# Normaliser states, conditioning vectors and a norm vector moved as rows with one transpose

## The chip, the cores and the metric

The kernel runs on one core of a Trainium2 chip. The core has five engines that work side by side: TensorE (PE) for matmuls and transposes, VectorE (DVE), ScalarE (ACT) and GpSimd (POOL) for elementwise work, and SyncE (SP), which here issues every transfer between device memory and the core's own memory (SBUF). PE writes into PSUM banks, which VectorE or ScalarE empty. The metric is the device time of one execution in microseconds, lower is better.

## The reference, cut to what matters

One layer of a diffusion backbone runs over 1024 sample tokens and 128 prompt tokens. A conditioning vector per group gives shifts and scales (`silu(c) @ w_mod + b_mod`). The mixer is a bidirectional mLSTM branch beside an attention branch; a feed-forward part follows. The mLSTM walks over the tokens in pieces and carries a matrix state C (256 x 256), a normaliser n (256) and a stabiliser m for each of 4 heads and 2 directions:

```python
num = w_inter[..., None] * jnp.einsum('bhid,bhde->bhie', qc, C) + jnp.einsum('bhij,bhje->bhie', s, vc)
den = w_inter * jnp.einsum('bhid,bhd->bhi', qc, n) + jnp.sum(s, -1)
h = num / jnp.maximum(jnp.abs(den), jnp.exp(-m_row))[..., None]
...
C_new = decay[..., None, None] * C + jnp.einsum('bhjd,bhje->bhde', wk, vc)
n_new = decay[..., None] * n + jnp.sum(wk, -2)
```

Sample tokens start from given states (`state_C`, `state_n`, `state_m`); prompt tokens start from zero, and their last states are outputs (`new_state_C`, `new_state_n` of shape 1 x 1 x 2 x 4 x 256, `new_state_m`). After the mLSTM each head's output is RMS-normalised and scaled by `mlstm_norm_g`, one number per channel.

## The kernel before, in words

**Layout.** The kernel keeps channels on the 128 partitions. A vector of 1024 numbers that is to lie with one number per partition and piece is read by the transfer in pieces of 4 bytes, since neighbours in memory go to different partitions. That holds for `mlstm_norm_g` into `mg` (line 393) and for each head's 256 numbers of `state_n` (line 514), and the other way for the final n into `o_n` (line 635). The conditioning vectors `c` and `c_ctx` lie with 8 neighbours on a partition, but go into `cT` with every second place (lines 298 and 299), again in pieces of 4 bytes. The modulation bias `b_mod` is read as 48 rows of 128 numbers into `bml` and transposed once on PE (line 330).

**A state tile.** C and n lie together in a tile `st` of 128 x 2 x 258: columns 0 to 255 are C, column 256 is n, column 257 is zero. The values `v` have a column of ones beside them, so one matmul group `kvp` updates C and n together. There are three `st` buffers in rotation.

**Stages.** Start (0 to about 60 us): modulation, transposes of x, gates. Then the mLSTM stage up to about 1000 us: `mlstm(h)` for the four heads in turn. Head h loads its backward state (`load_state(cur, h, 1)`), walks back over seven pieces and stores the state of each to device memory (`bs`), loads the forward state, and walks forward over eight sample pieces. The ninth piece is the prompt: for each direction its update is copied by ACT into an `st` buffer (`fin`, line 633) and stored, C in rows of 1 KB (`o_C`, line 634) and n from its column (`o_n`, line 635). `finish_h` transposes a piece's result on PE, scales it by `mg` on ACT (line 561) and stores it (`hmd`). Attention, the output projection and the feed-forward part follow.

**What sets the order.** `mlstm` is a generator. At each of its `yield`s the main loop takes a measured amount of other matmuls from `filler()` (projections `g`, copied out of PSUM by VectorE as `kvs` or `fm`, and late modulation pieces `mod_late`), so PE always has filler between the steps of the recurrence. The projections have two PSUM banks. A scheduler then fixes each engine's order once; an engine runs its list strictly in order. SP's list too: a transfer that has to wait holds all that come behind it. Transfers take their completion signals from a ring of eight, so each also waits until the eighth before it has landed.

**End of the mLSTM stage.** `prologue()` loads the keys `kTd` of the attention into `pe` tiles; ACT and VectorE split them into `kh` and `kl`. These loads stand on SP behind the last stores of the mLSTM stage.

**Statistics of the last norm.** `stats_act` uses four small tiles of 128 x 1, two buffers each.

Of the kernel before, what the change touches and what calls it, by code (L numbers as in the profile page):

```python
# [9 lines left out]
F32 = mybir.dt.float32  # L10
# [6 lines left out]
KT = 8  # L17
# [19 lines left out]
def hybrid_step_kernel(  # L37
# [27 lines left out]
    def load(out, in_):  # L65
        nc.sync.dma_start(out=out, in_=in_)

    def store(out, in_):
        nc.sync.dma_start(out=out, in_=in_)
# [63 lines left out]
    sc2p = cst.tile([128, 8, 2], F32, name="sc2p")  # L133
    bmT = cst.tile([128, 48], F32, name="bmT")
    silu = cst.tile([128, KT, 32], F32, name="silu")
    mg = cst.tile([128, 8], F32, name="mg")
    gq = cst.tile([128, 128], F32, name="gq")
    gk = cst.tile([128, 128], F32, name="gk")
    tmA = cst.tile([128, NT, 4, 4], F32, name="tmA")
# [46 lines left out]
    def ttile(shape):  # L186
        return ps1.tile(list(shape), F32, tag="t", bufs=1, name="pt")
# [106 lines left out]

    with ExitStack() as s0:
        p0 = pool(s0, "p0", 1)
        cT = p0.tile([128, KT, 2], F32, name="cT")
        load(cT[:, :, 0:1], c.rearrange("b (p k) -> p k b", k=KT))
        load(cT[:, :, 1:2], c_ctx.rearrange("(p k o) -> p k o", k=KT, o=1))
        sg = p0.tile([128, KT, 2], F32, name="sg")  # L300
        nc.scalar.activation(out=sg[:], in_=cT[:], func=AF.Sigmoid)
        nc.vector.tensor_tensor(out=silu[:, :, 0:2], in0=cT[:], in1=sg[:], op=ALU.mult)
        bml = p0.tile([48, 128], F32, name="bml")

        def mod_load(n, q):
            ch = p0.tile([128, 4, 512], F32, tag="ch", bufs=4, name="ch")
# [11 lines left out]

        c0 = [mod_load(0, q) for q in range(2)]
        load(sel[:], k_sel)  # L320
        load(bml[:], b_mod[0].rearrange("(j p) -> j p", p=128))
        load(ident[:], k_ident)
        c2 = [mod_load(2, q) for q in range(2)]
        load(wgr[:], kview(w_in)[:, :, GT:GT + 16])
# [1 line left out]
            load(bg[32 * j:32 * j + 4, :], b_gates[0, src:src + 4].rearrange("(p o) -> p o", o=1))  # L326
        for d in range(2):
            load(m0[32 * d:32 * d + 4, :], state_m[0, 0, d].rearrange("(p o) -> p o", o=1))
        pb = ttile([128, 48])
        nc.tensor.transpose(pb[:], bml[:], ident[0:48, 0:48])  # L330
        nc.vector.tensor_copy(out=bmT[:], in_=pb[:])
        mod_mm(0, c0)
        mod_mm(2, c2)
        nc.vector.tensor_scalar(sc1p[:, 0:4, :], modT[:, 8:12, :], 1.0, None, ALU.add)
# [55 lines left out]
            gate_mm(gg[b], b, range(4, KT), False, True)  # L390

    load(mask[:], k_mask)
    load(mg[:], mlstm_norm_g[0].rearrange("(k p) -> p k", p=128))
    load(gq[:], q_norm_g.partition_broadcast(128).rearrange("p o d -> p (o d)"))
    load(gk[:], k_norm_g.partition_broadcast(128).rearrange("p o d -> p (o d)"))
    nc.gpsimd.tensor_scalar(gq[:], gq[:], float(128.0 ** -0.5), None, ALU.mult)
# [92 lines left out]
    def mt(shape, tag, bufs=1, dt_=F32):  # L489
        return mp.tile(list(shape), dt_, tag=tag, bufs=bufs, name=tag)  # L490
# [20 lines left out]

    def load_state(dst, h, d):
        load(dst[:, :, 0:256], state_C[0, 0, d, h].rearrange("(k p) e -> p k e", p=128))
        load(dst[:, :, 256:257], state_n[0, 0, d, h].rearrange("(k p o) -> p k o", p=128, o=1))
        nc.gpsimd.memset(dst[:, :, 257:258], 0.0)

    def mlstm(h):
# [37 lines left out]
        def finish_h(s, hs):  # L555
            pt = ttile([128, 2, 128])
            for m in range(2):
                nc.tensor.transpose(pt[:, m, :], hs[:, 128 * m:128 * m + 128], ident[:])
            ho = mt([128, 2, 128], "ho", 2)
            for m in range(2):  # L560
                nc.scalar.activation(out=ho[:, m, :], in_=pt[:, m, :], func=AF.Copy, scale=mg[:, 2 * h + m:2 * h + m + 1])
            store(hmd[h][s][:], ho[:])
# [4 lines left out]
        for s in range(NT):  # L567
            sample = s < NS
            kv, v, uw, kT, pm = nxt_in
            qo = (s % 3) * 128  # L570
            q = qts[s // 3][:, :, qo:qo + 128]
            sp = ps1.tile([128, 512], F32, tag="s", bufs=1, name="sp")
            for m in range(2):
                nc.tensor.matmul(sp[:, 0:128], lhsT=kT[:, m, :], rhs=q[:, m, :], start=m == 0, stop=m == 1)
            sT = mt([128, 2, 128], "sT")
            nc.vector.tensor_tensor(out=sT[:], in0=sp[:, 0:128].unsqueeze(1).to_broadcast([128, 2, 128]), in1=pm[:], op=ALU.mult)
            sh, sl = mt([128, 2, 128], "sh", 1, F32R), mt([128, 2, 128], "sl", 1, F32R)
            split(sh[:], sl[:], sT[:])
            if sample:
                bw = mt([128, 2, 258], "bw", 2)  # L580
                load(bw[:], bsd[h][s][:])
                qw = mt([128, 2, 2, 128], "qw")
                nc.vector.tensor_tensor(out=qw[:], in0=q.unsqueeze(1).to_broadcast([128, 2, 2, 128]),
                                        in1=uw[:, 1, :, :].unsqueeze(2).to_broadcast([128, 2, 2, 128]), op=ALU.mult)
                qh, ql = mt([128, 2, 2, 128], "qh", 1, F32R), mt([128, 2, 2, 128], "ql", 1, F32R)
                split(qh[:], ql[:], qw[:])
                sts = []
                for nm, src in (("f", fw), ("b", bw)):
                    th, tl = mt([128, 2, 258], "sth" + nm, 1, F32R), mt([128, 2, 258], "stl" + nm, 1, F32R)
                    split(th[:], tl[:], src[:])  # L590
                    sts.append((th, tl))
            yield 1
            if pend is not None:
                finish_h(*pend)
            if s + 1 < NT:
                nxt_in = first(s + 1)
                yield 1
            op = ps1.tile([128, 2, 512], F32, tag="o", bufs=1, name="op")
            for d in range(2):
                terms = [((sh[:, d, :], sl[:, d, :]), (v[0][:], v[1][:]))]  # L600
                if sample:
                    terms += [((qh[:, d, m, :], ql[:, d, m, :]), (sts[d][0][:, m, :], sts[d][1][:, m, :])) for m in range(2)]
                mm3(op[:, d, 0:258], terms)
            r = mt([128, 2], "r", 2)
            nc.vector.tensor_tensor(out=r[:], in0=op[:, :, 256], in1=tmA[:, s, 2:4, h], op=ALU.max)
            nc.vector.scalar_tensor_tensor(out=r[:], in0=op[:, :, 256], scalar=-1.0, in1=r[:], op0=ALU.mult, op1=ALU.max)
            nc.vector.reciprocal(out=r[:], in_=r[:])
            ha = mt([128, 256], "ha")
            nc.scalar.activation(out=ha[:], in_=op[:, 0, 0:256], func=AF.Copy, scale=r[:, 0:1])
            hs = mt([128, 256], "hs", 2)  # L610
            nc.vector.scalar_tensor_tensor(out=hs[:], in0=op[:, 1, 0:256], scalar=r[:, 1:2], in1=ha[:], op0=ALU.mult, op1=ALU.add)
            ss = mt([128, 1], "ss", 2)
            jk = mt([128, 256], "jk")
            nc.scalar.activation(out=jk[:], in_=hs[:], func=AF.Square, scale=0.0625, accum_out=ss[:])
            nc.gpsimd.tensor_scalar(ss[:], ss[:], EPS, None, ALU.add)
            nc.gpsimd.tensor_tensor(out=ss[:], in0=ss[:], in1=mhalf[:, 0:1], op=ALU.pow)
            nc.vector.tensor_scalar(hs[:], hs[:], ss[:], None, ALU.mult)
            yield 1
            if sample:
                if s < NS - 1:  # L620
                    ps = kv_update(kv, v, h, s, 0)
                    nxt = mt([128, 2, 258], "st", 3)
                    for m in range(2):
                        nc.vector.scalar_tensor_tensor(out=nxt[:, m, :], in0=fw[:, m, :], scalar=dec[:, 0, h, s:s + 1],
                                                       in1=ps[m][:, 0:258], op0=ALU.mult, op1=ALU.add)
                    fw = nxt
                    yield 1
            else:
                for d in range(2):
                    ps = kv_update(kv, v, h, s, d)  # L630
                    fin = mt([128, 2, 258], "st", 3)
                    for m in range(2):
                        nc.scalar.activation(out=fin[:, m, :], in_=ps[m][:, 0:258], func=AF.Copy)
                    store(o_C[0, 0, d, h].rearrange("(k p) e -> p k e", p=128), fin[:, :, 0:256])
                    store(o_n[0, 0, d, h].rearrange("(k p o) -> p k o", p=128, o=1), fin[:, :, 256:257])
                    yield 1
            pend = (s, hs)
        finish_h(*pend)
        yield 1

# [515 lines left out]
        return nmu, rs, False  # L1156

    def stats_act(mk, y, jk):
        sm, nmu, ss, rs = (mk([128, 1], nm, 2) for nm in ("sm", "nmu", "sq", "brs"))
        nc.scalar.activation(out=jk, in_=y, func=AF.Copy, accum_out=sm[:])  # L1160
        nc.gpsimd.tensor_scalar(nmu[:], sm[:], -1.0 / D, None, ALU.mult)
        nc.scalar.activation(out=y, in_=y, func=AF.Identity, bias=nmu[:])
        nc.scalar.activation(out=jk, in_=y, func=AF.Square, accum_out=ss[:])
        nc.gpsimd.tensor_scalar(rs[:], ss[:], 1.0 / D, EPS, ALU.mult, ALU.add)
        nc.gpsimd.tensor_tensor(out=rs[:], in0=rs[:], in1=mhalf[:, 0:1], op=ALU.pow)
        return nmu, rs, True
# [334 lines left out]
```

## Time and profile before

| what | us |
|---|---|
| three runs | 2437.52, 2441.1, 2441.97 |
| median | 2441.1 |
| profiled execution, its own time | 2440.7 |
| its span, first to last instruction | 2438.9 |
| PE busy | 2360.1 (97%) |
| VectorE, ACT, POOL busy | 1495.6, 999.8, 366.6 |
| mean granted PE clock | 0.989 |
| PE busy in 0 to 60 us | 42.56 of 60 |
| PE busy in 300 to 400, 800 to 900, 1010 to 1100 us | 90.98 of 100, 91.38 of 100, 77.27 of 90 |

In the rows of the trace `out<-in` names what is written and read. L with a number is a line of the kernel before; lines 66 and 69 are the helpers `load` and `store`, 72 and 73 the helper `split`, 78 to 80 the three matmuls of `mm3`. `SPq` is SP's own queue. A wait row reads: who waited, for whom, us in total, times, longest. The windows give, for each stretch, length, busy time of PE, of PE's weight loads, VectorE, ACT and POOL with their instructions, then the granted PE clock (1 is full), the busy share of the 16 DMA engines and what they moved in GB/s.

### The profile page before, as it was taken

Reading aid. Unit: us, or ns where it says so; the run is one execution under the profiler, and the core shown is the slowest. Engines: PE = TensorE matmul, PEld = TensorE weight load, DVE = VectorE, ACT = ScalarE, POOL = GpSimd, SP = SyncE. Lnnn points to the kernel's source line nnn. Section 1 sums busy time; section 2 is a strip of 40 time slices with the busy share of each in tenths; the row PEclk is TensorE's granted clock in tenths of the full one; section 3 lists DMA queues with packets and bytes.
Section 4 is the critical chain, followed back from the end, with each engine's and each line's share of the span. In section 5 each row is a group of like instructions: output and inputs, shape, how many; then the busy total and the mean of one; then the engine's idle time right before and its main releaser. Section 6 shows DMA issues by size and latency. Waiting matters only on the chain.

```text
span 2438.9 us, 35985 instructions
## 1 busy us (share of the span) xinstructions
PE 2360.1 (97%) x13293; PEld 2135.6 (88%) x13293; DVE 1495.6 (61%) x2736; ACT 999.8 (41%) x2133; POOL 366.6 (15%) x566
## 2 busy tenths in 40 slices
PE   7999998999999899899999999999999999999997
PEld 4888887788899799898999999989999989999996
DVE  4745644745655455368788435679544587676777
ACT  3423432534433233246766423225433444444444
POOL 1000110201110011034444000010000121111111
PEclk9999999999999999999999999999999999999999
DMA  7265447445654653511000655434444452222222
GB/s 258 88 204 166 127 134 192 138 130 149 188 151 147 176 176 110 103 58 40 16 17 12 207 174 184 147 109 135 151 133 127 143 186 69 70 69 68 64 85 113
DMA packets 236849, 305.71 MB, mean 125 GB/s; under 512 B 25249, under 2 KB 175857, under 8 KB 236673
## 3 DMA queue, kind: packets, MB, share of 16 engines
q1 hardware_dynamic: 236672, 303.41, 41.2%
q8 instruction: 105, 1.72, 0.3%
q14 instruction: 72, 0.58, 0.1%
HBM read 236.55 MB, written 66.79 MB: 124 GB/s over the span
## 4 chain that ended last, share of the span: by engine, by line
PE 84%; DVE 6%; DMA 6%; ACT 2%; issue 1%; POOL 1%; SPq 0%; DVEq 0%; ACTq 0%; POOLq 0%
PE g L78 13%; PE g L80 13%; PE g L79 13%; PE u L1398 4%; PE d L78 3%; PE d L79 3%; PE d L80 3%; PE pz L1398 2%; PE pp L1398 2%; PE t L873 2%; PE u L80 2%; PE u L78 2%; PE u L79 2%; PE pa L79 2%; PE pa L80 2%; PE pa L78 2%
## 5 line engine op out<-in xcount | busy, mean ns | idle before, releaser
L78 PE MATMUL g<-th,wh 128*128 128x384 f32 x1088 | 373.6, 343 | 10.0 <-DVE fm L249 10.0
L80 PE MATMUL g<-th,wl 128*128 128x384 f32 x1088 | 368.2, 338 | 0.0
L79 PE MATMUL g<-tl,wh 128*128 128x384 f32 x1088 | 366.5, 337 | 0.0
L72 ACT ACTIVATE wh<-raw 128x1024 fp32r<-128x1024 f32 x180 | 188.7, 1057 | 316.2 <-PE d L80 142.3
L73 DVE TENSOR_TENSOR wl<-raw,wh 128x1024 fp32r<-128x1024 f32 x180 | 224.1, 1252 | 126.3 <-ACT wh L72 125.5
L78 PE MATMUL g<-wh,th 128*128 128x512 f32 x600 | 241.0, 402 | 0.3 <-DVE kvs L236 0.3
L79 PE MATMUL g<-wl,th 128*128 128x512 f32 x600 | 235.9, 393 | 0.2 <-DVE wl L73 0.2
L80 PE MATMUL g<-wh,tl 128*128 128x512 f32 x600 | 236.1, 394 | 0.0
L78 PEld LDWEIGHTS g<-th,wh 128*128 128x128 f32 x1088 | 206.4, 190 | 18.8 <-DVE fm L249 10.3
L79 PEld LDWEIGHTS g<-tl,wh 128*128 128x128 f32 x1088 | 206.5, 190 | 0.1
L80 PEld LDWEIGHTS g<-th,wl 128*128 128x128 f32 x1088 | 206.0, 189 | 0.4 <-issue 0.4
L1189 DVE TENSOR_TENSOR acc<-acc,d 128x512 f32<-128x512 f32 x160 | 109.5, 686 | 58.8 <-PE d L80 56.8
L78 PEld LDWEIGHTS g<-wh,th 128*128 128x128 f32 x600 | 113.1, 188 | 25.5 <-issue 3.8
L80 PEld LDWEIGHTS g<-wh,tl 128*128 128x128 f32 x600 | 113.0, 188 | 23.4
L79 PEld LDWEIGHTS g<-wl,th 128*128 128x128 f32 x600 | 113.2, 189 | 21.0 <-DVE wl L73 1.2
L72 ACT ACTIVATE ph<-t 128x384 fp32r<-128x384 f32 x192 | 91.0, 493 | 70.5 <-PE t L873 69.9
L249 DVE COPY fm<-g 128x384 f32<-128x384 f32 x96 | 53.2, 554 | 98.8 <-PE g L80 98.6
L73 DVE TENSOR_TENSOR pl<-t,ph 128x384 fp32r<-128x384 f32 x192 | 104.8, 549 | 9.0 <-ACT ph L72 7.2
L873 PE MATMUL t<-ident,pe 128*128 128x128 f32 x576 | 96.2, 276 | 6.3 <-DVE pl L73 5.4
L1302 POOL TENSOR_TENSOR wtl<-raw 128x512 f32<-128x512 f32 x16 | 21.2, 1324 | 487.4 <-PE pa L79 252.7
L862 POOL TENSOR_SCALAR pe<-pe,rs 128x1152 f32<-128x1152 f32 x64 | 79.0, 1234 | 54.8 <-DVE rs L861 26.9
L78 PE MATMUL pv<-ph,vh 128*128 128x256 f32 x288 | 85.6, 297 | 1.5 <-DVE tl L73 1.5
(392 smaller groups left out, 5905.5 us busy)
## 6 DMA issues: line engine op xcount, KB each, us to landing
raw<-in_w_up_dram SPq DMA_DIRECT2D x64, 512.0 KB
raw<-in_w_down_dram SPq DMA_DIRECT2D x64, 512.0 KB
raw<-in_w_in_dram SPq DMA_DIRECT2D x44, 512.0 KB
kvt<-kvd SPq DMA_DIRECT2D x64, 257.0 KB
raw<-in_w_mod_dram SPq DMA_DIRECT2D x32, 512.0 KB
kvd<-kvs SPq DMA_DIRECT2D x36, 257.0 KB
uw<-ud SPq DMA_DIRECT2D x72, 128.0 KB
bs<-st SPq DMA_DIRECT2D x32, 258.0 KB
```

Source lines behind the costliest of these rows:

```text
L72: nc.scalar.activation(out=hi, in_=src, func=AF.Copy)
L73: nc.vector.tensor_tensor(out=lo, in0=src, in1=f(hi), op=ALU.subtract)
L78: nc.tensor.matmul(out, lhsT=ah, rhs=bh, start=start and i == 0, stop=False)
L79: nc.tensor.matmul(out, lhsT=ah, rhs=bl, start=False, stop=False)
L80: nc.tensor.matmul(out, lhsT=al, rhs=bh, start=False, stop=stop and i == n - 1)
L249: nc.vector.tensor_copy(out=st[:], in_=g[:, 0:TB])
L862: nc.gpsimd.tensor_scalar(pe[:], pe[:], rs[:, 0:1], 1.0, ALU.mult, ALU.mult)
L873: nc.tensor.transpose(pt[:, k, :], pexp[u][:, kt * 128:kt * 128 + 128], ident[:])
L1189: nc.vector.tensor_tensor(out=y[:, cs], in0=y[:, cs], in1=g[:], op=ALU.add)
L1302: nc.gpsimd.tensor_tensor(out=tmp[i], in0=x, in1=y, op=op)
L1398: nc.tensor.matmul(o, lhsT=x[:, k, :], rhs=y[:, k, :], start=fresh and k == 0 and i == 0, stop=k == 3 and i == 2, skip_group_check=True)
```

## The change

`mg` becomes the first 8 columns of a tile `mgn` of 24 columns. The norm vector (8 rows) and `state_n` (16 rows) are loaded as rows of 128 numbers below the 48 rows of `b_mod`, and the one transpose there takes 72 rows. A second VectorE copy puts the 24 new columns into `mgn`. `load_state` takes n from `mgn` by a POOL copy; the eight `state_n` loads go. The prompt's final n is copied by POOL into the same columns of `mgn`; the eight `o_n` stores go. After the prompt piece of the last head one transpose turns these 16 columns into 16 rows, VectorE copies them to `no`, and one transfer stores them. `c` and `c_ctx` go into `cT` in whole pieces of 32 bytes, and VectorE reads them in the other order. Two of the small tiles of `stats_act` have one buffer.

```diff
-    mg = cst.tile([128, 8], F32, name="mg")
+    mgn = cst.tile([128, 24], F32, name="mgn")
+    mg = mgn[:, 0:8]
...
-        cT = p0.tile([128, KT, 2], F32, name="cT")
-        load(cT[:, :, 0:1], c.rearrange("b (p k) -> p k b", k=KT))
-        load(cT[:, :, 1:2], c_ctx.rearrange("(p k o) -> p k o", k=KT, o=1))
-        sg = p0.tile([128, KT, 2], F32, name="sg")
+        cT = p0.tile([128, 2, KT], F32, name="cT")
+        load(cT[:, 0, :], c.rearrange("b (p k) -> p (b k)", k=KT))
+        load(cT[:, 1, :], c_ctx.rearrange("(p k) -> p k", k=KT))
+        sg = p0.tile([128, 2, KT], F32, name="sg")
...
-        nc.vector.tensor_tensor(out=silu[:, :, 0:2], in0=cT[:], in1=sg[:], op=ALU.mult)
-        bml = p0.tile([48, 128], F32, name="bml")
+        nc.vector.tensor_tensor(out=silu[:, :, 0:2], in0=cT[:].rearrange("p j k -> p k j"),
+                                in1=sg[:].rearrange("p j k -> p k j"), op=ALU.mult)
+        bml = p0.tile([72, 128], F32, name="bml")
...
-        load(bml[:], b_mod[0].rearrange("(j p) -> j p", p=128))
+        load(bml[0:48, :], b_mod[0].rearrange("(j p) -> j p", p=128))
+        load(bml[48:56, :], mlstm_norm_g[0].rearrange("(j p) -> j p", p=128))
+        load(bml[56:72, :], state_n[0, 0].rearrange("d h (k p) -> (d h k) p", p=128))
...
-        pb = ttile([128, 48])
-        nc.tensor.transpose(pb[:], bml[:], ident[0:48, 0:48])
-        nc.vector.tensor_copy(out=bmT[:], in_=pb[:])
+        pb = ttile([128, 72])
+        nc.tensor.transpose(pb[:], bml[:], ident[0:72, 0:72])
+        nc.vector.tensor_copy(out=bmT[:], in_=pb[:, 0:48])
+        nc.vector.tensor_copy(out=mgn[:], in_=pb[:, 48:72])
...
-    load(mg[:], mlstm_norm_g[0].rearrange("(k p) -> p k", p=128))
...
-        load(dst[:, :, 256:257], state_n[0, 0, d, h].rearrange("(k p o) -> p k o", p=128, o=1))
+        nc.gpsimd.tensor_copy(out=dst[:, :, 256:257], in_=mgn[:, 8 + 8 * d + 2 * h:10 + 8 * d + 2 * h].unsqueeze(2))
...
-                    store(o_n[0, 0, d, h].rearrange("(k p o) -> p k o", p=128, o=1), fin[:, :, 256:257])
+                    nc.gpsimd.tensor_copy(out=mgn[:, 8 + 8 * d + 2 * h:10 + 8 * d + 2 * h], in_=fin[:, :, 256])
...
+        if h == NH - 1:
+            pt = ttile([16, 128])
+            nc.tensor.transpose(pt[:], mgn[:, 8:24], ident[:])
+            no = mt([16, 128], "no")
+            nc.vector.tensor_copy(out=no[:], in_=pt[:])
+            store(o_n[0, 0].rearrange("d h (k p) -> (d h k) p", p=128), no[:])
         finish_h(*pend)
...
-        sm, nmu, ss, rs = (mk([128, 1], nm, 2) for nm in ("sm", "nmu", "sq", "brs"))
+        sm, nmu, ss, rs = (mk([128, 1], nm, n) for nm, n in (("sm", 1), ("nmu", 2), ("sq", 1), ("brs", 2)))
```

The scheduler's order stays the same for most of the program. SP where head 0 hands over to head 1, before (`out_dram<-st 128x2x256` is `o_C`, `128x2x1` is `o_n`, `bs` the first state of head 1 on its way to device memory, `kvt` a piece of keys and values):

```order
L69 DMA kvd_7_123<-kvs 128x514
L69 DMA out_dram<-st 128x2x256
L69 DMA out_dram<-st 128x2x1
L66 DMA raw<-in_w_mod_dram 128x4x256
L66 DMA st<-in_state_C_dram 128x2x256
L69 DMA out_dram<-st 128x2x256
L69 DMA out_dram<-st 128x2x1
L69 DMA kvd_8_124<-kvs 128x514
L66 DMA st<-in_state_n_dram 128x2x1
L66 DMA raw<-in_w_mod_dram 128x4x256
L69 DMA hmd_8_154<-ho 128x256
L69 DMA bs_7_295<-st 128x516
```

And now:

```order
L69 DMA kvd_7_123<-kvs 128x514
L69 DMA out_dram<-st 128x2x256
L66 DMA raw<-in_w_mod_dram 128x4x256
L66 DMA st<-in_state_C_dram 128x2x256
L69 DMA out_dram<-st 128x2x256
L66 DMA raw<-in_w_mod_dram 128x4x256
L69 DMA kvd_8_124<-kvs 128x514
L69 DMA bs_7_295<-st 128x516
L66 DMA kvt<-kvd_4_111 128x514
L69 DMA hmd_8_154<-ho 128x256
```

Two stores and one load are gone, and the store of the first state stands four places earlier. POOL at the same place now has two copies into and two out of `mgn`, beside the memsets that stood there before:

```order
L639 COPY mgn<-st 128x2
L518 COPY st<-mgn 128x2
L519 MEMSET st 128x2
L639 COPY mgn<-st 128x2
L518 COPY st<-mgn 128x2
L519 MEMSET st 128x2
```

SP at the end of the mLSTM stage, before (`pe<-kTd` are the key loads of the attention):

```order
L69 DMA out_dram<-st 128x2x256
L69 DMA out_dram<-st 128x2x1
L69 DMA hmd_8_181<-ho 128x256
L69 DMA ga_0_250<-fm 128x384
L66 DMA pe<-kTd_202 128x256
L66 DMA pe<-kTd_203 128x256
```

And now:

```order
L69 DMA out_dram<-st 128x2x256
L69 DMA out_dram<-no 16x128
L69 DMA hmd_8_181<-ho 128x256
L69 DMA ga_0_250<-fm 128x384
L66 DMA pe<-kTd_202 128x256
L66 DMA pe<-kTd_203 128x256
```

The one row store stands where the last of the eight column stores stood, ahead of `hmd` as that did.

## Prediction

> **What bounds the kernel now.** I read the page's shares and chain first, then TensorE's waits over the whole span.
>
> ```profile
> PE 2360.1 (97%) x13293; PEld 2135.6 (88%) x13293; DVE 1495.6 (61%) x2736; ACT 999.8 (41%) x2133; POOL 366.6 (15%) x566
> PE 84%; DVE 6%; DMA 6%; ACT 2%; issue 1%; POOL 1%; SPq 0%; DVEq 0%; ACTq 0%; POOLq 0%
> PE kvp L78 <- DVE st L526: 11.2, 4, 8.6
> PE g L78 <- DVE fm L249: 10.0, 1, 10.0
> PE pm L314 <- DMA ch<-in_w_mod_dram: 10.1, 2, 9.4
> PE g L260 <- DVE fm L249: 8.8, 1, 8.8
> ```
>
> TensorE (PE) is busy 97% of the span, so only its gaps are to be had, and 6% of the chain is DMA. In the wait rows (total, times, longest) three single waits of 8.6 to 10.0 us stand out, after the start-up wait on `ch`. VectorE is named as releaser, but its own work there is short. So I asked for windows around the three, and around the one handover between heads that has no such wait. Columns: PE's busy time is the first number after the length; then the other engines, granted PE clock, DMA share, GB/s.
>
> ```profile
> 375.00:385.00 10.00, 1.22 (x11) 0.90 (x12) 2.02 (x5) 0.00 (x0) 0.00 (x0) 0.76 0.68 114
> 385.00:395.00 10.00, 10.00 (x55) 8.53 (x56) 5.83 (x13) 2.51 (x5) 0.00 (x0) 0.72 0.87 252
> 620.00:630.00 10.00, 7.39 (x37) 5.64 (x35) 6.12 (x14) 5.17 (x21) 2.31 (x4) 0.97 0.50 159
> 630.00:640.00 10.00, 10.00 (x44) 8.43 (x45) 9.06 (x22) 4.58 (x16) 0.30 (x1) 0.86 0.62 195
> 815.00:829.00 14.00, 5.38 (x32) 5.09 (x31) 1.91 (x5) 0.73 (x2) 0.00 (x0) 0.82 0.61 122
> 829.00:839.00 10.00, 10.00 (x49) 10.00 (x48) 5.28 (x14) 1.46 (x4) 0.00 (x0) 0.74 0.64 192
> 1013.00:1024.00 11.00, 0.97 (x7) 0.65 (x5) 1.81 (x4) 1.86 (x4) 0.38 (x2) 0.75 0.79 125
> 1024.00:1034.00 10.00, 10.00 (x45) 9.59 (x46) 4.74 (x7) 2.52 (x4) 1.85 (x3) 0.76 0.58 179
> ```
>
> Idle PE: 8.78, 2.61, 8.62 and 10.03 us, together 30.0. After each gap the granted clock is low for the next 10 us. Taking the missing part of the clock as lost work, (1 - 0.72) x 10 = 2.8, then 1.4, 2.6 and 2.4, together 9.2 us.
>
> What ends the gaps is in the chain (start, us, what) and in SP's waits from 1002 to 1021:
>
> ```profile
> 364.46 6.56 SPq L69
> 371.67 11.10 DMA st<-in_state_n_dram
> 382.89 0.88 DVE st L526 x2
> 601.69 9.50 DMA out_dram<-st
> 611.21 8.82 DMA st<-in_state_n_dram
> 620.99 2.26 DMA qTd<-qs
> 807.81 10.19 DMA out_dram<-st
> 818.01 9.51 DMA st<-in_state_n_dram
> 1001.05 18.66 DMA hmd<-ho
> SPq L66 <- DMA out_dram<-st: 13.1, 3, 8.7
> ```
>
> Each gap follows a `state_n` load, or at the end of the mLSTM stage an `hmd` store, that takes 9 to 19 us. Beside them a 256 KB store of long rows (`qTd`) lands in 2.26 us. In head 0 to 1 the SP queue itself is held for 6.56 us while it issues the second scattered store of the normaliser column (line 635), and so the `state_n` load starts late. `state_n` is 1 KB. What is ahead of it is the scattered store `o_n`, 256 pieces of 4 bytes:
>
> ```profile
> 366.00:370.00 4.00, 4.00 (x25) 3.96 (x24) 0.56 (x1) 0.63 (x2) 0.00 (x0) 1.00 0.60 25
> 616.00:619.00 3.00, 3.00 (x18) 2.56 (x18) 1.52 (x4) 1.33 (x3) 0.00 (x0) 1.00 0.56 21
> ```
>
> The 16 DMA engines are 56 to 60% busy and move 21 to 25 GB/s. In 385-395 they move 252 GB/s at a share of 0.87. That is what many tiny pieces look like. Loads of 4-byte pieces are not as slow: the two conditioning vectors are 2048 such pieces, the second issued at 1.44 us, and ScalarE (ACT), which needs them, starts at 4.4:
>
> ```profile
> 1.44 0.65 SPq L66 DMA_DIRECT2D cT<-in_c_ctx_dram  x1
> ACT L301 <- DMA cT<-in_c_ctx_dram: 4.4, 1, 4.4
> 3.00:6.00 3.00, 0.00 (x0) 0.00 (x0) 0.04 (x1) 1.50 (x2) 1.05 (x4) 1.00 0.92 197
> 6.00:9.00 3.00, 0.00 (x0) 0.00 (x0) 0.13 (x1) 0.00 (x0) 0.00 (x0) 1.00 0.98 341
> ```
>
> So I put the cost on the stores, with the loads queued behind them.
>
> **The change part by part.**
>
> *The scattered stores and loads of n.* Eight `o_n` stores and eight `state_n` loads go. What is left at a handover is the load of `state_C`:
>
> ```profile
> 362.71 0.50 SPq L66 DMA_DIRECT2D st<-in_state_C_dram  x1
> 606.79 0.43 SPq L66 DMA_DIRECT2D st<-in_state_C_dram  x1
> 811.67 0.38 SPq L66 DMA_DIRECT2D st<-in_state_C_dram  x1
> ```
>
> SP then reaches the next instruction without the 6.56 us hold. The first state of a head is whole when `state_C` has landed: issued at 362.71 in head 0 to 1, some 13 us before PE runs dry (1.22 us of work are left after 375). VectorE can do `st` L526 right behind the first `kvp` group instead of at 382.89, and the copies of `g` behind it no longer hold PE's banks. What is late next is the store of `o_C` in 1 KB rows, which shares its buffer. By the 2.26 us row it lands some 10 us before it is needed, and at 9.5 us, the length of the scattered one, still 2 us before. For heads 0 to 1 and 2 to 3 I take the whole 8.78 + 8.62 = 17.4, with 2.8 + 2.6 = 5.4 of clock. For head 1 to 2 I take half of 2.61 + 1.4, that is 2.0, because the q/k preparation on POOL and VectorE runs into the same place. Bounds: 0 (all of it something else's) and 26.8.
>
> *The end of the mLSTM stage.* There VectorE stands behind the split of the first keys (`kTd`), and SP's loads of these wait for the two `o_n` stores and then for the `hmd` store behind them in the rings. Now one store of 16 rows of 512 B stands in the place of the last two. Its chain is ACT's copy, one POOL copy, one transpose, one VectorE copy. The `hmd` store was issued at 1001.05. I put both stores at 1001 to 1002.5, landed by 1005 at 2.26 us each. The key loads (eight issues of about 0.4 us) follow by 1008, and VectorE is free before PE's two banks run out at 1013.9. Gain 10.0 + 2.4 = 12.4; bounds 0 and 12.4.
>
> *Clock after the gaps.* The Trainium skill, "TensorE: Matmul & The Clock Gate", section "What's actually happening", has half rate after an idle window and full rate after some 3.4 us of sustained work. By it each long gap would cost about 1.7 us, an estimate from that page. The rows show 2.4 to 2.8, longer than the rule. With the rule the sum would be some 3 us smaller; I go by the rows.
>
> *Start.* The vectors `c` and `c_ctx` go from 2048 pieces to 256. The 3-6 us window moves 197 GB/s at a share of 0.92, the next one 341 at 0.98. Against that rate some 3 x (1 - 197/341) = 1.3 us are missing, in part plain start latency. PE's first matmuls wait 9.4 us for `ch` behind them. Two row loads are new, in front of `ident` and the second pair of `ch`, and the transpose at line 330 needs them:
>
> ```profile
> 3.92 0.75 SPq L66 DMA_DIRECT2D bml<-in_b_mod_dram  x1
> 4.71 0.43 SPq L66 DMA_DIRECT2D ident<-in_k_ident_dram  x1
> 13.91 0.34 PE L330 MATMUL pt<-ident,bml 48*128 48x48 f32 x1
> ```
>
> They push `ident` back by 2 x 0.4 to 0.75 us on a queue with some 9 us to spare. Gain 0.7; bounds 0 and 1.3. The load of `mg` (1024 pieces) goes too, at 42.6 us, where nothing on the path stands behind it: 0.
>
> *What is added.*
>
> ```profile
> L338 POOL COPY wz<-wgr 128x32 f32<-128x32 f32 x4 | 0.7, 212 | 14.2 <-DMA wgr<-in_w_in_dram 14.2
> L439 POOL COPY MI<-m 36x1 f32<-36x1 f32 x1 | 1.0, 1020 | 0.0
> L331 DVE COPY bmT<-pt 128x48 f32<-128x48 f32 x1 | 0.2, 198 | 0.0
> ```
>
> Sixteen POOL copies of two columns, 0.2 to 1.0 us each, 3.4 to 16.3 us in all, on an engine that is 15% busy. They stand where a memset of the same tile stood already, so SP's `bs` store, which waits for POOL and holds all later loads, waits no longer than one copy more. The `mgn` copy at the start (0.2) is on the path, since the next `modt` needs its bank. The last transpose takes the single `t` bank from `finish_h`: a copy of 0.2 us and the way there and back against three matmuls between, 0.3 us. Sum 0.5. One buffer instead of two for `sm` and `sq` costs nothing: POOL reads each at once, long before the next token writes it.
>
> *Sum.* 17.4 + 5.4 + 2.0 + 12.4 + 0.7 - 0.5 = 37.4. The profiled execution took 2440.7 us (span 2438.9), 0.4 under the median of 2441.1. 2440.7 - 37.4 = 2403.
>
> **Rivals.**
>
> *The end gap stays* (2403 + 12.4 = 2415). SP's key loads wait for stores eight issues back, and the new store stands in front of `hmd`. If it is late, the sixth key load is, and VectorE stays blocked. For it: four copies and transposes in a row feed it. Against it: it would have to land after 1011, nine microseconds after its issue.
>
> *Nothing but the start moves* (2440). If a scattered 1 KB store costs what any small store does, the clog is `o_C`'s or the weights' and the gaps stay. For it: `o_C` goes out just ahead of each `o_n`, and no row times one without the other. Against it: 21 GB/s at a share of 0.56 in 616-619. The Trainium skill, "DMA: Bandwidth & Descriptors", section "Anatomy of one DMA", gives a fixed 2 us and a part that goes by bytes. By that rule a 1 KB store would be no slower than others; the same page's "Rules for kernel authors" has a strided last dim become one descriptor per element.
>
> *Slower: POOL is now in every handover.* A state tile is whole only after POOL's copy, which stands in POOL's order behind the pow operations that wait for ACT:
>
> ```profile
> POOL qss L650 <- ACT qjk L649: 23.4, 5, 10.3
> ```
>
> It decides from where the copy comes later than `state_n` landed: 371.67 + 11.10 - 362.71 = 20 us after the issue of `state_C` in the first handover, 13 and 16 in the others. At 5 us beyond that in three handovers and in the last store, the time is 2440.7 + 20 = 2461. POOL's longest wait around the second handover, 10.3 us, stays short of it.
>
> **How the numbers follow.** Forecast 0.76, own range 2397 to 2411 (head 1 to 2 whole or nothing, the start 0 or 1.3, the clock by half). End gap stays 0.13. Nothing moves 0.07. Slower 0.03. 0.01 is left for more than I see. A measurement of this kernel tells 0.2% from no change, 5 us. Faster 0.90, same 0.07, slower 0.03. Range 2395 to 2421: it takes in the forecast and the end gap.
>
> **What would show it.** Right: no PE wait above 3 us between 60 and 1100 us; clock 1.00 at the handovers; `st` L526 a few us after the first `kvp` of a head; the `kTd` loads issued within 8 us of the last `hmd`; the span's loss at four places, little elsewhere. Wrong: a DMA share above 0.5 at under 30 GB/s behind the `o_C` stores; SP held at L69 there; VectorE waiting for POOL's `st` copy; or gaps of the same length at another load.

## The result, and the profile after

The changed kernel takes 2399.1 us (median of 4 runs, 2398.0 to 2401.2) against 2439.3 us beside it: a ratio of 0.9836, 95% interval 0.9819 to 0.9853, or 40.0 us (36 to 44) at 2441 us. The forecast was 2403, with 37.4 us gained. The profiled execution took 2398.0 us (span 2396.2).

In rows of the changed kernel and of the runs below, L with a number is a line of that kernel. The page's shares of the engines:

```profile
PE 2348.3 (98%) x13294; PEld 2125.0 (89%) x13294; DVE 1494.3 (62%) x2738; ACT 999.6 (42%) x2133; POOL 372.0 (16%) x582
```

TensorE's waits between 60 and 1100 us, the costliest (total, times, longest):

```profile
PE t L883 <- DVE pl L73: 2.3, 5, 1.2
PE pt L550 <- ACT ho L565: 1.6, 3, 0.8
PE pt L683 <- ACT kT L552: 1.6, 1, 1.6
```

The waits of 8.6 to 10.0 us are gone; the longest left is 1.6. Everything now runs earlier than before, by some 4, 15, 20 and 31 us at the four places where TensorE had run dry (the marks below). The same windows view of the second `o_C` store of head 0 and of these four places, shifted by as much:

```profile
360.00:365.00 5.00, 5.00 (x30) 4.89 (x30) 1.31 (x4) 0.63 (x3) 0.00 (x0) 1.00 1.07 368
370.00:375.00 5.00, 5.00 (x36) 4.34 (x35) 2.56 (x8) 0.73 (x2) 0.00 (x0) 1.00 0.73 209
375.00:385.00 10.00, 10.00 (x68) 9.34 (x67) 7.09 (x15) 3.58 (x6) 0.00 (x0) 1.00 0.90 256
606.00:616.00 10.00, 10.00 (x54) 8.50 (x53) 8.00 (x18) 4.02 (x14) 2.28 (x4) 1.00 0.60 178
800.00:810.00 10.00, 10.00 (x68) 9.33 (x67) 6.46 (x17) 2.19 (x6) 0.00 (x0) 1.00 0.50 157
975.00:985.00 10.00, 10.00 (x60) 9.97 (x59) 4.52 (x7) 2.69 (x5) 2.24 (x4) 1.00 0.54 157
985.00:995.00 10.00, 10.00 (x60) 10.00 (x59) 4.90 (x6) 3.17 (x4) 1.91 (x2) 1.00 0.51 159
```

PE is busy throughout these windows, the granted clock is 1.00, and behind the second `o_C` store (360 to 365) the DMA engines move 368 GB/s where they moved 25.

Where the time went is read by marks that both programs have: ACT's final copy of the states (`st<-kvp`, once per head and direction and half; the first one of heads 0, 1 and 2 and the last one of head 3 mark the head's end) and the first transpose of the keys in attention (`t<-ident,pe`). First and last start of these groups, before and after:

```profile
L633 ACT ACTIVATE st<-kvp x16: 367/384/390, 358.2 to 998.1; 128x258 f32<-128x258 f32 x16
L873 PE MATMUL t<-ident,pe x576: 270/272/331, 1063.0 to 1348.9; 128*128 128x128 f32 x192
```

```profile
L637 ACT ACTIVATE st<-kvp x16: 368/384/389, 353.9 to 966.6; 128x258 f32<-128x258 f32 x16
L883 PE MATMUL t<-ident,pe x576: 270/272/329, 1019.1 to 1305.9; 128*128 128x128 f32 x192
```

With the first ones of heads 1 and 2 (600.7 and 805.8 before, 585.9 and 785.8 after) this gives, in us:

| stretch | before | after | gained | forecast |
|---|---|---|---|---|
| start to end of head 0 | 358.2 | 353.9 | 4.3 | 0.7 - 0.2 |
| handover 0 to 1, head 1 | 242.5 | 232.0 | 10.5 | 8.8 + 2.8 |
| handover 1 to 2, head 2 | 205.1 | 199.9 | 5.2 | 2.0 |
| handover 2 to 3, head 3 | 192.3 | 180.8 | 11.5 | 8.6 + 2.6 |
| end of mLSTM to attention | 64.9 | 52.5 | 12.4 | 12.4 - 0.3 |
| attention to the end | 1375.9 | 1377.1 | -1.2 | 0 |
| sum | 2438.9 | 2396.2 | 42.7 | 37.4 |

PE's busy time between the same marks tells idle time from slower work, since the number of matmuls differs by two at most. In the four rows from the first handover to the start of attention PE is idle for 7.9, 2.6, 8.6 and 10.0 us less, and busy for 2.6, 2.6, 2.9 and 2.4 us less (230.37 to 227.78, 202.49 to 199.90, 182.93 to 180.04, 54.87 to 52.50).

### The profile page after: what moved, and what is told of

The parts are those of the page before. It is cut to its first block, busy times and chain, and to the rows that moved or that the text cites. A ratio compares the mean times of both kernels' runs of the same rounds, so it can differ in the third digit from the quotient of the medians.

```text
span 2396.2 us, 36004 instructions
## 1 busy us (share of the span) xinstructions
PE 2348.3 (98%) x13294; PEld 2125.0 (89%) x13294; DVE 1494.3 (62%) x2738; ACT 999.6 (42%) x2133; POOL 372.0 (16%) x582
## 4 chain that ended last, share of the span: by engine, by line
PE 87%; DVE 6%; DMA 3%; ACT 2%; issue 1%; POOL 1%; SPq 0%; DVEq 0%; ACTq 0%; POOLq 0%
PE g L78 14%; PE g L80 13%; PE g L79 13%; PE u L1408 4%; PE d L78 3%; PE d L79 3%; PE d L80 3%; PE pp L1408 3%; PE pz L1408 3%; PE t L883 2%; PE u L80 2%; PE u L78 2%; PE u L79 2%; PE pa L79 2%; PE pa L80 2%; PE pa L78 2%
```

## Experiments

All were timed beside the kernel before, in four groups with a "before" of their own each, so the ratios are compared. "Cost" is (ratio - 0.9836) x 2441 us, what the run lost against the changed kernel; with both intervals it is uncertain by about 5 us, so "costs nothing" below means nothing beyond that.

| run | us | ratio (95%) | cost, us |
|---|---|---|---|
| stores of n scattered again | 2439.9 | 0.9981 (0.9972-0.9990) | 35 |
| loads of n scattered again | 2400.9 | 0.9826 (0.9812-0.9839) | -2 |
| before, conditioning vectors alone | 2439.3 | 0.9985 (0.9976-0.9994) | |
| + 256 pieces of 512 B | 2399.3 | 0.9821 (0.9806-0.9836) | -4 |
| + 256 pieces of 4 B, 512 B apart | 2401.3 | 0.9831 (0.9816-0.9845) | -1 |
| + 256 pieces of 64 B | 2398.8 | 0.9822 (0.9807-0.9837) | -3 |
| + 128 pieces of 4 B, side by side | 2434.0 | 0.9961 (0.9948-0.9973) | 31 |
| stores scattered, on ACT's queue | 2435.9 | 0.9974 (0.9963-0.9985) | 34 |
| + 256 pieces of 32 B | 2398.6 | 0.9835 (0.9820-0.9850) | 0 |
| + 256 pieces of 4 B, 64 B apart | 2400.8 | 0.9846 (0.9831-0.9860) | 2 |
| + 256 of 4 B side by side, last head | 2409.4 | 0.9883 (0.9867-0.9900) | 11 |
| + 256 pieces of 16 B | 2400.9 | 0.9831 (0.9814-0.9848) | -1 |

**The stores back, the loads back.** The two halves of the change on n, each undone alone. In the first, line 639 is the store again and the block at `h == NH - 1` goes; in the second, line 518 is the load again.

```
-  nc.gpsimd.tensor_copy(out=mgn[:, 8 + 8 * d + 2 * h:...], in_=fin[:, :, 256])
+  store(o_n[0, 0, d, h].rearrange("(k p o) -> p k o", p=128, o=1), fin[:, :, 256:257])
```

```
-  nc.gpsimd.tensor_copy(out=dst[:, :, 256:257], in_=mgn[:, 8 + 8 * d + 2 * h:...].unsqueeze(2))
+  load(dst[:, :, 256:257], state_n[0, 0, d, h].rearrange("(k p o) -> p k o", p=128, o=1))
```

> The changed kernel, in which only the eight scattered stores of n come back (256 pieces of 4 bytes each, where they stood); the loads of n stay in one row, and the transpose at the end goes. Theory (the stores clog, the loads only queued behind them): at the end of the mLSTM stage the hmd store and the key loads stand behind the last two stores again, so the gap of about 10 us and its 2.4 us of clock return; at the handovers nothing of the state is queued behind them now, but SP is held again, so between nothing and the 27 us gained there return. 2399 + 12 to 2399 + 39, likeliest 2425. Rival (the 4-byte loads are what takes 9 to 11 us): no gap at all, 2399 to 2401.

> The changed kernel, in which only the eight scattered loads of n come back; the stores stay in one row. Theory (stores clog): without the stores ahead of them the loads land in a few us, no PE wait above 3 us between 60 and 1100 us, 2399 to 2402. Rival (the loads are slow by themselves): st in the first step of a head waits 8 to 10 us again at three handovers, 2399 + 27 = 2426, while the end of the mLSTM stage stays clean.

The stores alone bring back 35 of the 40 us; the loads alone bring back nothing that can be measured. The forecast's cause holds, and at the top end of what was expected: I had thought that some of the handovers would stay clean with no load of n behind the stores. They don't. From the chain of waits of the run with the stores back (start, us, what), in the first handover and at the end of the mLSTM stage:

```profile
365.73 17.78 DMA out_dram<-st
383.57 4.08 DMA kvt<-kvd
...
1001.75 17.06 DMA hmd<-ho
1019.72 2.17 DMA pe<-kTd
```

SP's issue of the second `o_C` store with the scattered one behind it, and two windows of the same run:

```profile
365.29 6.57 SPq L69 DMA_DIRECT2D out_dram<-st  x2
```

```profile
366.00:372.00 6.00, 6.00 (x37) 5.96 (x36) 1.33 (x3) 0.63 (x2) 0.00 (x0) 1.00 0.60 45
820.00:830.00 10.00, 1.87 (x10) 1.58 (x9) 1.56 (x5) 0.00 (x0) 0.00 (x0) 0.75 0.64 144
```

SP is held for 6.57 us over these two issues (before, 6.99 over the same two), a store takes 17.78 us, and now the next thing in the line, the load of k and v (`kvt`, 4.08 us), is what VectorE waits for. PE is dry for nearly as long as before: 8.13 us of the 10 in 820 to 830 (8.62 in 815 to 829 before). The load of n was only the first in line. In the run with the loads back, the longest wait of PE between 60 and 1100 us is 1.2 us:

```profile
PE t L883 <- DVE pl L73: 2.1, 4, 1.2
PE pt L550 <- ACT ho L565: 1.6, 3, 0.8
```

**The start alone.** The kernel before with the changed lines 298 to 304 only.

> The kernel before, in which only the two conditioning vectors are loaded in 32-byte pieces (256 instead of 2048). The events of the changed kernel run 2.2 us earlier at the first matmul and 4.3 to 4.6 us earlier by the end of the start. Theory (all of that is from these two loads): 2439.3 - 4.4 = 2435. Rival (the forecast's term was right, and the rest is from the clock of that one execution or from the other row loads): 0.7 to 1.3 us, 2438 to 2439.

It gains 0.15% (0.06 to 0.24), 3.7 us (1.5 to 5.9): more than the forecast's bound of 1.3. The 4.3 of the profiled execution is not a better number; part of it is luck. It had a clock of 1.00 in the first 60 us, other executions with the same start 0.94 to 0.97, and the first `st<-kvp` of these comes at 354.4 to 360.3, in the mean of these twelve at 356.6, 2.7 us later than in that one execution. What repeats is the first matmul, at 9.38 in the one trace before, 7.76 here and 7.1 to 7.6 in nearly all runs of the changed start (8.47 in one). From PE's order of time, ACT's waits and the windows of this run:

```profile
7.76 1.94 PE L315 MATMUL pm<-ch,silu 128*32 128x512 f32 x8 [7.76 <-DMA ch<-in_w_mod_dram]
```

```profile
ACT L301 <- DMA cT<-in_c_ctx_dram: 3.0, 1, 3.0
```

```profile
3.00:6.00 3.00, 0.00 (x0) 0.00 (x0) 0.18 (x1) 1.47 (x2) 1.04 (x4) 1.00 0.84 284
6.00:9.00 3.00, 1.24 (x8) 0.23 (x8) 0.00 (x0) 0.00 (x0) 0.00 (x0) 1.00 1.05 388
```

The vectors are there 1.4 us earlier, and the first matmul starts 1.6 us earlier. How the other 2 us of the timed gain come about is not settled; with an interval of 1.5 to 5.9 they need not be there at all.

**How many pieces, how many bytes.** The changed kernel, and behind each `o_C` store one more store in 256 pieces, as many as a store of n has, to a scratch buffer `px`: of 512, 64, 32 or 16 bytes, side by side. For 64 bytes (the others differ in the two sizes):

```
+  px = [[dr.tile([2, 128, 16], F32, name=f"px{h}_{d}") for d in range(2)] for h in range(NH)]
...
+  store(px[h][d][:].rearrange("k p e -> p k e"), fin[:, :, 240:256])
```

> The changed kernel, and behind each store of o_C one more store of 256 pieces, of 512 bytes each, to a scratch buffer that nothing reads: as many pieces as a scattered store of n, 128 times the bytes. Theory (the pieces of 4 bytes cost, not their number): each lands in 2 to 4 us like other 128 KB stores, 2399 to 2403. Rival (the number of pieces costs): as with the scattered stores back, 12 to 39 us more, 2411 to 2438.

> As the run with 512-byte pieces (2399.3), with 256 pieces of 64 bytes side by side in a scratch buffer. Theory A (a small piece is slow by its size, and 64 bytes are small): 2430 to 2442. Theory B (only pieces that share a short stretch of memory with their neighbours collide, which these do less than those of 4 bytes): 2399 to 2408.

> As the run with 256 pieces of 64 bytes side by side (2398.8), with pieces of 32 bytes side by side (the side-by-side pieces of 4 bytes cost 41 us). Theory A (pieces are in each other's way when two of them lie in the same 64 bytes): a clear part of the 41 us, 2406 to 2440. Theory B (the stretch in which they collide is 32 bytes or less): 2398 to 2402.

> As the run with pieces of 32 bytes side by side (2398.6), with pieces of 16 bytes. Theory A (pieces collide when two lie in the same 32 bytes): with two instead of eight to such a stretch, a part of the 41 us, 2403 to 2436. Theory B (it takes more neighbours than two, or a shorter stretch): 2398 to 2402.

None costs anything that can be measured. So it is not the number of pieces alone, and down to 16 bytes it is not their size.

**Pieces of 4 bytes, but not side by side.** The n column itself to a scratch buffer, every piece 512 or 64 bytes from the next (`px` is 2 x 128 x 128 or 2 x 128 x 16 numbers, and each piece fills the first number of a row):

```
+  store(px[h][d][:, :, 0:1].rearrange("k p e -> p k e"), fin[:, :, 256:257])
```

> The changed kernel, and behind each store of o_C a store of the n column in 256 pieces of 4 bytes to a scratch buffer that nothing reads, each piece 512 bytes from the next (in o_n they lie side by side). With the eight scattered stores of n alone back the time was 2439.9, some 41 us above the changed kernel. Theory A (a piece of 4 bytes is slow wherever it goes): the same again, 2432 to 2442. Theory B (pieces that lie side by side in memory are in each other's way): 2399 to 2408.

> As the run with pieces of 4 bytes 512 bytes apart (2401.3), with 64 bytes from one to the next. Theory A (the stretch in which pieces collide is 64 bytes or less): 2398 to 2403. Theory B (it is longer than 64 bytes; the run with 64-byte pieces was clean since each filled its stretch, not since it was alone there): 2406 to 2440.

This is the sharpest comparison. Both runs and the one with the stores back write eight times 256 pieces of 4 bytes right behind the `o_C` stores. The page's packets, first with the stores back, then 512 bytes apart (under 512 B they differ by 15):

```profile
DMA packets 231889, 305.71 MB, mean 125 GB/s; under 512 B 20265, under 2 KB 170897, under 8 KB 231713
```

```profile
DMA packets 231920, 305.72 MB, mean 128 GB/s; under 512 B 20280, under 2 KB 170928, under 8 KB 231744
```

SP's issues of these stores in the first handover, 512 bytes apart, and a window:

```profile
356.64 0.51 SPq L69 DMA_DIRECT2D px<-st  x1
361.47 0.46 SPq L69 DMA_DIRECT2D px<-st  x1
```

```profile
361.00:363.00 2.00, 2.00 (x13) 1.88 (x12) 1.49 (x4) 0.32 (x2) 0.19 (x1) 1.00 1.04 360
```

512 bytes apart the issue takes 0.46 to 0.51 us instead of some 6.1 (the 6.57 above hold an issue of `o_C` too, 0.4), the engines move 360 GB/s right around the second store, and the time is 2401.3 instead of 2439.9. What costs is that pieces of 4 bytes lie side by side in memory. The run with the stores back differs from these two in more: it writes the output itself, and lacks POOL's copies of the final n and the last transpose. The next run and that of the last head write side by side into a scratch buffer with all of these in place, and are held up as well.

**Half as many, side by side.** 128 pieces of 4 bytes, in 512 bytes of scratch.

```
+  store(px[h][d][0:1, :, :].rearrange("k p e -> p k e"), fin[:, 0:1, 256:257])
```

> The changed kernel, and behind each store of o_C a store of only the first 128 of the 256 pieces of 4 bytes, to a scratch buffer, side by side. If the cost goes by the number of pieces, such a store lands in half the 9 to 18 us, and the time is 2399 plus 10 to 20, 2409 to 2419. If a few such pieces already stop the queue, 2430 to 2440. If there is slack enough for half, 2399 to 2403.

Half the pieces cost 31 of the 35 us, as in the second branch of what was expected; the 10 to 20 are refuted, so the cost doesn't go by the number of pieces. It is no clean count: here most of these stores are issued just ahead of the `o_C` store, not behind it. In the chain one such store of half a kilobyte takes 9.19 us, and the load of weights behind it 13.38:

```profile
355.85 9.19 DMA px<-st
365.06 13.38 DMA raw<-in_w_mod_dram
```

**Another queue.** The run with the stores back, with the scattered stores of n issued by ACT.

```
-  store(o_n[0, 0, d, h]..., fin[:, :, 256:257])
+  nc.scalar.dma_start(out=o_n[0, 0, d, h]..., in_=fin[:, :, 256:257])
```

> The kernel with the eight scattered stores back (2439.9), with those stores issued by ACT on its own queue instead of by SP. Theory A (the stores are in the way of what is behind them in the same queue): the loads pass them, 2399 to 2406. Theory B (the 16 DMA engines themselves are clogged for all queues): no better than on SP, 2430 to 2442. If ACT is held at the issue as SP was (6.57 us), its copies for PE come late and the time lies between, 2406 to 2430.

34 us: no better than on SP within the intervals. ACT issues in 0.48 us, and SP is held at a load of weights that has nothing to do with n; a store ends 16.16 us later. ACT's and SP's issues, then the chain:

```profile
366.16 0.48 ACTq L639 DMA_DIRECT2D out_dram<-st  x1
366.63 6.36 SPq L66 DMA_DIRECT2D raw<-in_w_mod_dram  x1
```

```profile
366.16 16.16 DMA out_dram<-st
```

So what is held up is shared by these two queues. The Trainium skill, "DMA: Bandwidth & Descriptors", section "Issuing engines are not separate DMA queues", says that issuing from several engines saves only the time of the issue; this run agrees.

**The last head alone.** Side-by-side stores of n to scratch only where `h == NH - 1`.

> The changed kernel, and in the last head alone two stores of 256 pieces of 4 bytes side by side, to a scratch buffer, where the scattered stores of n stood. Theory (the forecast's term for the end of the mLSTM stage, 10.0 of gap and 2.4 of clock, is from these two): 2399.1 + 12.4 = 2411, and the handovers between heads stay clean. Rival (the row store in front of hmd, or the transpose, had its part in it, or the gap needs the earlier stores too): 2399 to 2405.

11 us (6 to 17), against a forecast of 12.4 for this place. PE's costliest wait between 60 and 1100 us, the chain and the windows show the old end gap, and no other:

```profile
PE g L78 <- DVE fm L251: 8.3, 1, 8.3
```

```profile
967.71 17.51 DMA px<-st
985.23 3.03 DMA pe<-kTd
```

```profile
975.00:985.00 10.00, 7.48 (x44) 7.16 (x42) 0.00 (x0) 0.00 (x0) 0.00 (x0) 1.00 0.99 123
985.00:995.00 10.00, 4.18 (x13) 3.77 (x14) 4.31 (x7) 2.68 (x5) 2.23 (x4) 0.51 0.58 167
```

The gap costs the 2.52 and 5.82 us that PE is idle, and the clock in 985 to 995 is 0.51. The row store and the last transpose, which this run keeps, don't make the gap: the changed kernel has them and no gap, and the run with the stores back has the gap without them.

## Why the prediction was right, step by step

- **The gaps are the time to be had, and the stores make them.** Right. Stores back: 35 us at the four places (by the marks against the changed kernel 9.6, 5.9, 11.1 and 9.9). Loads back: none. The two halves don't share the gain: the rows for the loads are worth 0.0004 (the ratio of the start alone, less that of the stores back), 1 us, within the uncertainty.
- **"That is what many tiny pieces look like."** The right stores, but too wide a reason. As many pieces of 4 bytes, 512 or 64 bytes apart, cost nothing, and the engines move 360 GB/s around them. Here it took pieces of 4 bytes that are neighbours in memory. The change takes these stores away whatever the reason is, so the forecast's number says nothing for this remark.
- **"The load of state_n queued behind them."** Right for the kernel before, but the load is not a necessary link. With it gone, `kvt` or the next load takes its place. The prediction's remark that the state is whole when `state_C` has landed would, without the store's part of the change, have been worth nothing (1 us in the run with the stores back).
- **Heads 0 to 1 and 2 to 3, 22.8 with the clock.** Measured 10.5 + 11.5 = 22.0; in the first of the two PE's idle time fell by 7.9 of the 8.78. In head 1 the first `st` comes at 368.46, 0.6 us behind the first `kvp`, where it came at 382.89.
- **Head 1 to 2, 2.0.** Mis-sized: 5.2, and 5.9 in the run with the stores back. The step that failed is the half taken off for the q/k preparation: with the stores gone, PE is busy from 606 to 616 without a break. The whole gap and its clock would have been 4.0. The other 1.2 lies in PE's busy time, which fell by 2.6 us where the rows gave 1.4 of clock; why it fell by that much is open.
- **End of the mLSTM stage, 12.4.** Measured 12.4 by the marks and 11 by the run of the last head alone. SP's issues show the steps as forecast:

```profile
969.10 0.34 SPq L69 DMA_DIRECT2D out_dram<-no  x1
970.26 0.33 SPq L69 DMA_DIRECT2D hmd<-ho  x1
971.16 2.32 SPq L66 DMA_DIRECT2D pe<-kTd  x5
975.24 2.51 SPq L66 DMA_DIRECT2D pe<-kTd  x3
```

  The eight key loads are out 7.5 us behind the issue of the last `hmd` (8 were promised).
- **Clock after the gaps, by the rows.** Right. At the three long gaps the rows gave 2.8, 2.6 and 2.4 us, and PE's busy time fell by 2.6, 2.9 and 2.4, together 7.9 against 7.8. By the rule of the Trainium skill, "TensorE: Matmul & The Clock Gate", section "What's actually happening", with the estimate of 1.7 us a gap that the prediction worked out from it, they would be 5.1. The measurement decides for the rows, and the trace of the kernel before agrees: in windows of 1 us the granted clock stays at 0.50 for 5.5, 6.0 and 4.9 us after PE resumes.
- **Start, 0.7 (0 to 1.3).** Mis-sized: 3.7 (1.5 to 5.9), of which 1.6 stands at the first matmul. The step that failed is the reference: the window 6 to 9 us, 341 GB/s, was taken as unhindered, but with the change it moves 386 to 388 GB/s. By 388, the two windows lacked 3 x (1 - 197/388) + 3 x (1 - 341/388) = 1.8 us, near the 1.6.
- **Added, 0.5; POOL.** Not to be seen apart: from the start of attention to the end the changed kernel takes 1.2 us more, 1377.1, where the profiled executions of the other runs take 1375.4 to 1379.5. The load of `mg` and the single buffers of `sm` and `sq` were not run apart. No engine waits for POOL's state copy (line 518 of the changed kernel); the slower rival on POOL falls, as do "the end gap stays" and "nothing but the start moves". The fixed 2 us that the last one takes from the Trainium skill, "DMA: Bandwidth & Descriptors", section "Anatomy of one DMA", is a fit for transfers that GpSimd issues; SP issues all of these stores.

Against the two profiled executions the sum was 5.3 us too small: 3.8 at the start and 3.2 in head 1 to 2, and -1.1, 0.3, 0.3 and -1.2 elsewhere. Of the 3.8, 2.7 are the luck of one execution (above). Against the timed runs it was 2.6 too small, inside their interval.

## What to carry to other kernels

A store that puts single 4-byte elements of many partitions side by side into memory is to be looked for first wherever the trace shows a high DMA share at a few tens of GB/s: what shows as late is whatever load or store comes next, here also one from another queue. Making the victims leaner bought nothing here (1 us for the loads of n); turning the column into rows on the chip and storing once did (one transpose and one store stand for 35 us). Read the gain of such a change off the gaps themselves, and take no window beside a disturbance as the undisturbed rate.

## What the runs showed of the hardware

- 256 pieces of 4 bytes side by side in 1 KB came with transfers of 9 to 19 us, their own or those behind them (8.82 to 18.66 in the kernel before, 17.78 with the stores back, 17.51 in the last head alone). 512 or 64 bytes apart, or as 16, 32, 64 or 512 bytes side by side, 256 pieces cost nothing that could be measured. The Trainium skill, "DMA: Bandwidth & Descriptors", section "Rules for kernel authors", has a strided last dimension become one descriptor per element. By that alone the runs with 256 pieces of 4 bytes would be alike; they differ by 33 to 36 us.
- The Trainium skill, "Collectives: The Full Stack", section "Rules for kernel authors", asks for 32-byte alignment of the buffers of collectives, which spares the hardware a read-modify-write. No run here shows such writes. If such writes are behind this, a lone partial write is not dear (4 bytes at 64-byte steps: 2400.8), nor are two pieces to 32 bytes (16-byte pieces: 2400.9). Eight pieces to 32 bytes were. Whether it is the number of pieces in a short stretch, or that all of them fall into one kilobyte, stays open: pieces of 16 bytes cover 4 KB as well as being fewer to a stretch, and no run separates the two. So what exactly collides was not shown.
- Half the pieces cost almost as much (31 against 35 us). Why was not settled either.
- In the kernel before, after idle gaps of 8.6 to 10 us the granted clock was 0.50 for the next 4.9 to 6.0 us of PE's work. With the gaps gone, PE's busy time at each of the three places is 2.4 to 2.9 us shorter.
